# Second weights of the channel sub-layer in the buffers of the other half's input, loaded and split two steps ahead

## The chip, the cores and the metric

The kernel runs on one core of a Trainium2 chip. The metric is the device time of one execution in microseconds (us). A core has five engines that run their own instruction queues in order and wait for each other by semaphores: TensorE (PE in the profile; its weight loads are PEld), VectorE (DVE), ScalarE (ACT), GpSimd (POOL) and SyncE (SP), which here only issues transfers. Matrix products are accumulated in PSUM; everything else lies in SBUF.

## The reference

One layer of a decoder for 1024 prompt tokens and 8 sample tokens, each sample with 8192 cached positions. Its first sub-layer mixes tokens (stick-breaking attention, over a paged cache for the samples, and gated linear attention). Its second, the channel sub-layer, is the one that is changed:

```python
h2 = modulate(x1, sh2, sc2)                      # (tokens, 1024)
f = jnp.square(jax.nn.relu(h2 @ w_ff1)) @ w_ff2  # 1024 -> 4096 -> 1024
x2 = layer_norm(ALPHA * x1 + gt2 * f, ln2_g, ln2_b)
```

All arrays are float32.

## The kernel before, in words

**Products in three parts.** Each factor of a large product is split into a high part (a copy rounded to fp32r, by ACT, L313) and a low part (the rest, by POOL or DVE, L314), and the product is the sum of high x high, low x high and high x low. `three` puts the matmuls in that order, so a weight's low part is needed in the last third.

**The channel sub-layer** is `ffn(n, ...)`, run for the first half of the prompt (n = 0, 512 tokens) and then for the second (n = 1, with the 8 sample tokens beside it). The 4096 hidden units are 32 blocks of 128, taken in pairs. An *up* step (24 matmuls into `pmm`) makes one block's hidden values, which ACT evacuates (`rl`, L1502), DVE squares (L1503) and both split (`hidh`, `hidl`). A *down* step multiplies a pair's hidden values by two second weights: 4 token tiles x 2 halves of the columns, 6 matmuls each, in the PSUM tiles `pz` and `ptr`; DVE adds each to `f` (L1550). The steps go up, up, down, the down lagging one pair: A B | A' B' down(A,B) | A'' B'' down(A',B') ... The last down of a half is followed tile by tile by the gate (`tmpf`, L1554), the LayerNorm and the store; in the second half it takes four blocks, two of them in a wide buffer.

**Weights.** `load_split` fetches a block into a raw buffer by SP (`wf`, 512 KB), ACT writes its high part and POOL its low part. All of `raw` (6 buffers) and `whi` (3 buffers) are shared: first weights use a raw buffer, a high and a low one (the low ones are `raw` too), and so do second weights. Each step's weights are asked for while the step before is written out:

```python
        ws = yield from load(*steps[0])
        for y, (x, us) in enumerate(steps[:-1]):
            nxt = yield from load(*steps[y + 1])
```

**The input of the sub-layer.** `second_in(n, h2, alloc)` reads the first sub-layer's result back, normalizes it (L1382), transposes it on TensorE (`pT`), scales and shifts it (L1393) and splits it into 8 high and 8 low tiles. The first half's lie in the 16 buffers `b1`, the second half's in the 16 buffers `b2`. The second half's input is made as a task of its own soon after the first half's:

```python
        yield from mix_out(1, mhb, ws, lambda: flow.spawn(second_in(0, h2a, b1)))
        flow.spawn(second_in(1, h2b, b2), 60.0)
        yield from ffn(0, h2a, False)
```

**What sets the order.** The program is written out by generators whose tasks interleave by a clock counted in matmuls; a scheduler then orders each engine's instructions by that priority and by when buffers come free. The samples' attention over the cache runs as such tasks beside the first half's sub-layer: POOL issues the gathers of cache rows (`kt`, `vt`, 1 MB each, L636), DVE multiplies and reduces keys (L659, L661), TensorE multiplies values (`va`), and at the end transposes sums (`posT`, `pups`).

Of the kernel before, what the change touches and what calls it, by code (L numbers as in the profile page):

```python
# [12 lines left out]
F32R = mybir.dt.float32r  # L13
# [7 lines left out]
P = 128  # L21
# [14 lines left out]
A_LAG, A_PACE, B_LAG, SG_MAX = 6.5, 7.0, 2.0, 6  # L36
N_HK, N_MID, N_RAW, N_W, N_KV = 9, 9, 6, 3, 3
GATES_EARLY = 10
N_FA, N_DK = 8, 4
E_LAG = 2.0  # L40
U_LEAD = 7.2
SCALE = 1.2
# [74 lines left out]
def tile_trunk_step(ctx: ExitStack, tc: tile.TileContext, i: dict, o: dict):  # L117
# [4 lines left out]
    sb = ctx.enter_context(tc.tile_pool(name="sb", bufs=1))  # L122
# [8 lines left out]
    def fa(shape, name, dt=F32):  # L131
        return sb.tile(list(shape), dt, tag="fa", name=name, bufs=N_FA)

    def b1(name):
        return sb.tile([P, 512], F32R, tag="b1", name=name, bufs=16)

    def b2(name):
        return sb.tile([P, 512], F32R, tag="b2", name=name, bufs=16)

    def small(shape, name, dt=F32):  # L140
        return sb.tile(list(shape), dt, tag="small", name=name, bufs=5)
# [25 lines left out]
    flow = Flow()  # L167
# [83 lines left out]
    for c in range(2):  # L251
        t = cp.tile([P, 8], F32, name=f"sel2_{c}")
# [156 lines left out]
        yield 0.0  # L409


    hhi = [[(b1, b2)[n](f"hhi{k}_{n}") for n in range(2)] for k in range(8)]
    hlo = [[(b1, b2)[n](f"hlo{k}_{n}") for n in range(2)] for k in range(8)]
    hsT = cp.tile([P, 8, 32], F32, name="hsT")
    V.memset(hsT, 0.0)

# [772 lines left out]
    def mix_in(n):  # L1189

        ohl = []
        for x in range(2):
            for k in range(4):
                r = (hk if n else mid)([P, 512], "or")
                nc.sync.dma_start(r, d_o[x][k][n])
                h, lo = b1("oh"), b1("ol")
                split(r, h, lo, V)
                ohl.append((h, lo))
        return ohl

    def mix_up(n, ohl, mh):

        stage[0] = 2

        def fetch_up(m):
            r = raw([P, 2, 4, P], "ru")
            for x in range(2):
                fetch(r[:, x], w_up[x][:, P * m : P * m + P].rearrange("(k p) c -> p k c", p=P), U_LEAD)
            return r

        def load(m, r):
            wh = sb.tile([P, 2, 4, P], F32R, tag="whi", name="wuh", bufs=N_W)
            wl = sb.tile([P, 2, 4, P], F32R, tag="raw", name="wul", bufs=N_RAW)
            split(r, wh, wl)
            gs = []
            for x in range(2):
                g = hk([P, 512], "g")
                nc.sync.dma_start(g, d_br[x][m][n])
                gs.append(g)
            return wh, wl, gs  # L1220


        rr = [fetch_up(0)]
        nxt = load(0, rr[0])
        rr.append(fetch_up(1))
        for m in range(8):
            wh, wl, gs = nxt
            if m < 6:
                rr.append(fetch_up(m + 2))
            nxt = load(m + 1, rr[m + 1]) if m < 7 else wo_tiles(0)  # L1230
            for x in range(2):
                p = p_big(x)
                steps = three([(ohl[4 * x + k], (wh[:, x, k, :], wl[:, x, k, :])) for k in range(4)])
                for y, (h, wt) in enumerate(steps):
                    mm(p, wt, h, start=y == 0, stop=y == 11)
                    if y == 5:
                        yield
                V.tensor_tensor(gs[x], gs[x], p, ALU.mult)
                yield
            V.tensor_tensor(gs[0], gs[0], gs[1], ALU.add)  # L1240
            h, lo = b2("mh"), b2("ml")
            split(gs[0], h, lo)
            mh.append((h, lo))
        return nxt
# [130 lines left out]
    def second_in(n, h2, alloc):  # L1375

        for hf in range(2):
            xs = []
            for t in range(4):
                x = hk([P, 512], "x1")  # L1380
                nc.sync.dma_start(x, d_x1[4 * n + t][:, 512 * hf : 512 * hf + 512])
                V.tensor_scalar(  # L1382
                    x, x, x1_mu[:, 2 * t : 2 * t + 1, n], x1_mu[:, 2 * t + 1 : 2 * t + 2, n], ALU.subtract, ALU.mult
                )
                xs.append(x)
            yield 9.0
            for kk in range(4):
                k = 4 * hf + kk
                p = p_tr([P, 4, P], "pT2")
                for t in range(4):  # L1390
                    turn(p[:, t, :], xs[t][:, P * kk : P * kk + P], ident)
                t = hk([P, 512], "h2")
                V.tensor_scalar(  # L1393
                    t, p.rearrange("p a b -> p (a b)"), ada_col("sc2", k), ada_col("sh2", k), ALU.mult, ALU.add
                )
                h, lo = alloc("h2h"), alloc("h2l")
                split(t, h, lo)
                h2.append((h, lo))
                yield 1.5
        done.add(("h2", n))  # L1400

    def ffn(n, h2, smpl):


        NU = DFF // P
# [102 lines left out]
        def load_down(us):  # L1508
            ws = []
            wide = []  # L1510
            for x, u in enumerate(us):
                dst = None
                if x >= 2:
                    if not wide:
                        for nm in ("wwh", "wwl"):
                            wide.append(sb.tile([P, 2, 2, 512], F32R, tag="kv", name=nm, bufs=N_KV))
                    dst = wide[0][:, x - 2], wide[1][:, x - 2]
                go = hid[u][2]
                if go is not None:
                    yield lambda: bool(go)  # L1520

                def use(r, go=go):
                    held2.append(r)
                    if len(held2) == 2:
                        smp_down(held2, go)
                        held2.clear()

                ws.append(load_split(
                    w_ff2[P * u : P * u + P, :].rearrange("p (a b) -> p a b", a=2), 2, 512, "wf2",
                    None if go is None else use, dst,  # L1530
                ))
            return ws
# [33 lines left out]
        def load(x, us):  # L1566
            if us is None:
                return load_up(x)
            return (yield from load_down(us))
# [13 lines left out]
            store(y_s, xs, 8, nc.sync)  # L1583


        ws = yield from load(*steps[0])
        for y, (x, us) in enumerate(steps[:-1]):
            if smpl and y == len(steps) - 2:
                ln2 = rows(i["ln2_g"][0]), rows(i["ln2_b"][0])
                flow.spawn(smp_end())  # L1590
            nxt = yield from load(*steps[y + 1])
            if us is None:
                yield from up(x, *ws)
            else:
                for t in range(4):
                    for cc in range(2):
                        add_up(f[t][cc], down_tile(us, ws, t, cc), x == 0)
                        yield
            ws = nxt
        us = groups[-1]  # L1600
        for t in range(4):
            xs = halves(d_x1[4 * n + t], P, "xf")
            for h in range(2):
# [27 lines left out]
    def main():  # L1631
# [13 lines left out]
        yield from mix_out(0, mha, ws, lambda: o1.extend(mix_in(1)))  # L1645
        ws = yield from mix_up(1, o1, mhb)
        yield from mix_out(1, mhb, ws, lambda: flow.spawn(second_in(0, h2a, b1)))
        flow.spawn(second_in(1, h2b, b2), 60.0)
        yield from ffn(0, h2a, False)
        yield from ffn(1, h2b, True)  # L1650

# [75 lines left out]
```

## Time and profile before

| | |
|---|---|
| runs timed: median (lowest to highest of 3) | 2135.22 us (2133.79 to 2137.54) |
| the profiled execution, its own time | 2129.62 us |
| its span, first to last instruction | 2127.9 us |
| mean granted TensorE clock | 0.961 of full speed |
| busy: TensorE, its weight loads | 1954.9 us (92%), 1372.5 us |
| busy: VectorE, ScalarE, GpSimd | 1460.7, 709.9, 909.7 us |

The busy time is a sum over all stages. Engines wait at different places in each, so the stretches of the channel sub-layer (from about 1220 us) have to be read one by one; idle time of an engine that nobody waits for costs nothing.

### The profile page before, as it was taken

What the parts mean: (1) busy time and instruction counts of PE and PEld (TensorE: products, weight loads), DVE (VectorE), ACT (ScalarE), POOL (GpSimd) and SP (SyncE); (2) the same over time, 40 slices, a digit from 0 to 9 for tenths busy, and PEclk for the clock granted to TensorE, in tenths of its full rate; (3) what the DMA queues carried; (4) which work ended last, traced back from release to release, by engine and by line L of the source; (5) the groups of instructions that cost most, each with busy time, mean ns of one, the idle gap of its engine ahead of it and who ended that gap; (6) DMA issues with size and microseconds to landing.
All of it is one profiled execution on the core that took longest, in us unless ns stands there. A gap on an engine that the chain in (4) does not pass through costs nothing.

```text
span 2127.9 us, 28882 instructions
## 1 busy us (share of the span) xinstructions
PE 1954.9 (92%) x11300; PEld 1372.5 (64%) x11300; DVE 1460.7 (69%) x1770; ACT 709.9 (33%) x1152; POOL 909.7 (43%) x615
## 2 busy tenths in 40 slices
PE   5899999998899989888898889999999899999996
PEld 2776765665556656656876666676766666667774
DVE  6477888797777788656897989987335644333347
ACT  2333544553426533222232333222221432222222
POOL 2342233334334323327475657555444533234335
PEclk8998999999999889999999999999999999999998
DMA  7785578787778668798987888878668454443232
GB/s 263 245 303 179 183 259 271 254 272 265 264 260 297 224 206 301 283 343 287 338 316 259 279 275 299 284 281 300 206 203 279 147 159 125 134 132 106 80 99 102
DMA packets 270083, 498.06 MB, mean 234 GB/s; under 512 B 16006, under 2 KB 198630, under 8 KB 234107
## 3 DMA queue, kind: packets, MB, share of 16 engines
q0 software_dynamic: 36864, 268.45, 34.9%
q1 hardware_dynamic: 205538, 199.17, 29.7%
q10 hardware_dynamic: 27544, 28.59, 3.8%
q8 instruction: 89, 1.46, 0.3%
q14 instruction: 48, 0.39, 0.1%
HBM read 465.45 MB, written 30.71 MB: 233 GB/s over the span
## 4 chain that ended last, share of the span: by engine, by line
PE 49%; DVE 18%; DMA 14%; issue 11%; POOL 4%; ACT 3%; SPq 0%; DVEq 0%; ACTq 0%; POOLq 0%
PE pmm L189 21%; PE pz L189 7%; PE ptr L189 7%; DMA kt<-in_cache_k,idx 5%; DVE z L661 3%; PE pbig L189 3%; PE va L189 3%; DVE kt L659 3%; PE pfs L189 2%; DMA vt<-in_cache_v,idx 2%; DVE kp L772 2%; DMA wo<-in_w_o 1%; DMA wbr<-in_w_in 1%; DMA wf<-in_w_ff 1%; DVE xr L1299 1%
## 5 line engine op out<-in xcount | busy, mean ns | idle before, releaser
L659 DVE TENSOR_TENSOR kt<-kt,qb 128x2048 f32<-128x2048 f32 x128 | 291.5, 2278 | 80.9 <-DMA kt<-in_cache_k,idx 78.1
L661 DVE TENSOR_REDUCE z<-kt 128x32 f32<-128x2048 f32 x128 | 291.5, 2280 | 1.2
L636 POOL DMA_INDIRECT vt<-in_cache_v,idx x128 | 132.2, 1033 | 306.9 <-PE va L189 129.1
L636 POOL DMA_INDIRECT kt<-in_cache_k,idx x128 | 133.4, 1043 | 282.5 <-DVE z L661 102.0
L314 POOL TENSOR_TENSOR wfl<-wf,wfh 128x1024 fp32r<-128x1024 f32 x64 | 155.4, 2429 | 206.2 <-ACT wfh L313 187.5
L314 POOL TENSOR_TENSOR wf2l<-wf,wf2h 128x1024 fp32r<-128x1024 f32 x62 | 150.6, 2430 | 113.7 <-ACT wf2h L313 91.2
L313 ACT ACTIVATE wfh<-wf 128x1024 fp32r<-128x1024 f32 x64 | 67.5, 1055 | 269.5 <-PE ptr L189 142.4
L189 PE MATMUL pmm<-h2h,wfh 128*128 128x512 f32 x512 | 144.1, 415 | 11.7 <-DVE rl L1503 4.2
L189 PE MATMUL va<-vt,wT 128*8 128x512 f32 x1024 | 141.7, 619 | 13.7 <-DMA vt<-in_cache_v,idx 13.5
L189 PE MATMUL pmm<-h2l,wfh 128*128 128x512 f32 x512 | 137.5, 401 | 0.4 <-POOL h2l L314 0.4
L1503 DVE TENSOR_TENSOR rl<-rl,pmm 128x512 f32<-128x512 f32 x64 | 43.7, 682 | 134.8 <-ACT rl L1502 134.5
L189 PE MATMUL pmm<-h2h,wfl 128*128 128x512 f32 x512 | 132.5, 395 | 0.0
L189 PEld LDWEIGHTS pmm<-h2h,wfh 128*128 128x128 f32 x512 | 95.1, 194 | 56.9 <-issue 22.0
L1550 DVE TENSOR_TENSOR f<-f,pz 128x512 f32<-128x512 f32 x108 | 73.9, 684 | 70.5 <-PE pz L189 69.3
L189 PEld LDWEIGHTS pmm<-h2l,wfh 128*128 128x128 f32 x512 | 95.2, 189 | 31.1 <-issue 9.7
L189 PEld LDWEIGHTS pmm<-h2h,wfl 128*128 128x128 f32 x512 | 94.9, 188 | 26.1 <-issue 6.0
L1550 DVE TENSOR_TENSOR f<-f,ptr 128x512 f32<-128x512 f32 x108 | 73.9, 684 | 44.2 <-PE ptr L189 43.5
L772 DVE TENSOR_TENSOR_SCAN kp<-kp,zcol 128x512 f32<-128x512 f32 (+3 forms) x96 | 99.9, 1052 | 2.6 <-ACT kp L765 1.4
L189 PE MATMUL pz<-wf2h,hidh 128*128 128x512 f32 x248 | 83.5, 405 | 10.9 <-DVE tmpf L1554 4.5
L1502 ACT ACTIVATE rl<-pmm 128x512 f32<-128x512 f32 x64 | 38.2, 597 | 164.5 <-PE pmm L189 161.1
L314 DVE TENSOR_TENSOR hidl<-rl,hidh 128x512 fp32r<-128x512 f32 x64 | 79.0, 1234 | 15.9 <-ACT hidh L313 15.7
L189 PE MATMUL pz<-wf2l,hidh 128*128 128x512 f32 x248 | 82.1, 400 | 6.0 <-POOL wf2l L314 5.9
(431 smaller groups left out, 4248.0 us busy)
## 6 DMA issues: line engine op xcount, KB each, us to landing
wf<-in_w_ff SPq DMA_DIRECT2D x128, 512.0 KB
ra<-in_w_ada SPq DMA_DIRECT2D x24, 1024.0 KB
wfs<-in_w_ff SPq DMA_DIRECT2D x20, 512.0 KB
wbr<-in_w_in SPq DMA_DIRECT2D x16, 512.0 KB
d_br<-brg ACTq DMA_DIRECT2D x32, 256.0 KB
g<-d_br SPq DMA_DIRECT2D x32, 256.0 KB
wo<-in_w_o SPq DMA_DIRECT2D x16, 512.0 KB
xt<-in_x_prompt SPq DMA_DIRECT2D x8, 512.0 KB
```

The costliest lines, as they stand in the source:

```text
L189: ins = E.matmul(out, lhsT, rhs, start=start, stop=stop, **kw)
L313: S.activation(hi, src, AF.Copy)
L314: (eng or G).tensor_tensor(lo, src, hi.bitcast(F32), ALU.subtract)
L636: G.indirect_dma_start(t, None, src, bass.IndirectOffsetOnAxis(ap=idx[:, 16 * b + j : 16 * b + j + 1], axis=0))
L659: dot = V.tensor_tensor(k3, k3, qb[:, None, :].to_broadcast([P, 4, 512]), ALU.mult)
L661: V.tensor_reduce(z[:, :, :, j], kt.rearrange("p (r h d) -> p r h d", r=4, h=8), AX.X, ALU.add)
L772: V.tensor_tensor_scan(kp[:, 0:w][:, ::-1], kp[:, 0:w][:, ::-1], zcol.to_broadcast([P, w]), init, ALU.mult, ALU.max)
L1299: V.scalar_tensor_tensor(xr[t][hf][:, cs], xr[t][hf][:, cs], ALPHA, tmp, ALU.mult, ALU.add)
L1502: S.activation(rl, p, AF.Relu)
L1503: V.tensor_tensor(rl, rl, p, ALU.mult)
L1550: V.tensor_tensor(f, f, p, ALU.add)
```

## The change

The 16 single buffers of `b1` and of `b2` become 8 double ones each; inputs take a high and a low half of one. A second weight takes two of them (a whole one for its high part, one for its low): in the first half of the sub-layer from `b2`, for all pairs but the last three, in the second half from `b1`. Such a down step's weights are loaded and split two steps ahead, so together with those of the second up. The second half's input, which needs `b2`, is made when only the last three pairs of the first half are left.

```diff
-N_FA, N_DK = 8, 4
+N_FA, N_DK, N_LAST = 8, 4, 6
...
+    def pair(tag, name):
+
+        t = sb.tile([P, 2, 512], F32R, tag=tag, name=name, bufs=8)
+        return t[:, 0, :], t[:, 1, :]
+
     def b1(name):
-        return sb.tile([P, 512], F32R, tag="b1", name=name, bufs=16)
+        return pair("b1", name)
...
-                h, lo = alloc("h2h"), alloc("h2l")
+                h, lo = alloc("h2")
                 split(t, h, lo)
...
                 dst = None
+                if x < 2 and (n or us[0] < NU - N_LAST):
+
+                    dst = tuple(
+                        sb.tile([P, 2, 512], F32R, tag=("b2", "b1")[n], name=nm, bufs=8) for nm in ("wf2h", "wf2l")
+                    )
...
-        ws = yield from load(*steps[0])
+        ahead_ = [(yield from load(*steps[0]))]
+
+        def early(y):
+            us = steps[y][1] if y < len(steps) else None
+            return us is not None and len(us) == 2 and (n == 1 or us[0] < NU - N_LAST)
+
         for y, (x, us) in enumerate(steps[:-1]):
...
-            nxt = yield from load(*steps[y + 1])
+            while len(ahead_) < min(len(steps), y + (3 if early(y + 2) else 2)):
+                ahead_.append((yield from load(*steps[len(ahead_)])))
+            ws = ahead_[y]
+            if n == 0 and y == len(steps) - 3 * N_LAST // 2 + 1:
+                flow.spawn(second_in(1, h2b, b2))
...
-        flow.spawn(second_in(1, h2b, b2), 60.0)
         yield from ffn(0, h2a, False)
```

What it does to the order on the engines, at the three places that matter. First TensorE at the seam of the two halves: the last two token tiles of the first half's last down (`pz`, `ptr`), the cached values (`va`) and the first up of the second half (`pmm`). Before:

```order
L189 MATMUL pz<-wf2h,hidh 128x512 x2
L189 MATMUL pz<-wf2h,hidl 128x512 x2
L189 MATMUL pz<-wf2l,hidh 128x512 x2
L189 MATMUL ptr<-wf2h,hidh 128x512 x2
L189 MATMUL ptr<-wf2h,hidl 128x512 x2
L189 MATMUL ptr<-wf2l,hidh 128x512 x2
L189 MATMUL va<-vt,wT 8x512 x8
L189 MATMUL pmm<-h2h,wfh 128x512 x8
```

Now (the input's tiles are named `h`), after 16 matmuls of the up with `wfh`:

```order
L194 MATMUL pmm<-h_12769,wfl 128x512
L194 MATMUL pmm<-h_12802,wfl 128x512
L194 MATMUL pmm<-h_12822,wfl 128x512
L194 MATMUL pz<-wf2h,hidh 128x512 x2
L194 MATMUL pz<-wf2h,hidl 128x512 x2
L194 MATMUL pz<-wf2l,hidh 128x512 x2
L194 MATMUL ptr<-wf2h,hidh 128x512 x2
L194 MATMUL ptr<-wf2h,hidl 128x512 x2
L194 MATMUL ptr<-wf2l,hidh 128x512 x2
L194 MATMUL pmm<-h_12853,wfl 128x512
```

The 24 matmuls of the first up have moved ahead of the last two token tiles, 19 before the third and 5 before the fourth. Second ACT in the second half, one pair of blocks with the sample rows' partial sums (`partf`) between. Before:

```order
L313 ACTIVATE wfh<-wf 128x1024 x2
L1442 ACTIVATE partf<-pfs_14609 128x256
L1442 ACTIVATE partf<-pfs_14656 128x256
L1502 ACTIVATE rl<-pmm 128x512
L313 ACTIVATE hidh<-rl 128x512
L313 ACTIVATE wf2h<-wf_14692 128x1024
L1502 ACTIVATE rl<-pmm 128x512
L313 ACTIVATE wf2h<-wf_14698 128x1024
L313 ACTIVATE hidh<-rl 128x512
```

Now:

```order
L318 ACTIVATE wfh<-wf 128x1024
L1448 ACTIVATE partf<-pfs_14545 128x256
L318 ACTIVATE wf2h<-wf_14568 128x1024
L318 ACTIVATE wf2h<-wf_14574 128x1024
L1448 ACTIVATE partf<-pfs_14608 128x256
L1508 ACTIVATE rl<-pmm 128x512
L318 ACTIVATE hidh<-rl 128x512
L318 ACTIVATE wfh<-wf 128x1024
L1508 ACTIVATE rl<-pmm 128x512
L318 ACTIVATE hidh<-rl 128x512
```

Both high parts of the second weights now stand ahead of the up's evacuation and between the two `partf`; a first weight has moved behind it. Third DVE at the seam, behind the masked copy of the cached values' sum (`vz`). Before:

```order
L738 COPY_PREDICATED vz<-hmask,va 128x512
L304 RECIPROCAL rs<-rs 128x1
L1620 SCALAR_TENSOR_TENSOR nm<-mv,rs 128x1
L299 BN_STATS st<-f_10304 128x6
L299 BN_STATS st<-f_10305 128x6
L1623 TENSOR_TENSOR f_10302<-f_10302,row 128x512
L1623 TENSOR_TENSOR f_10303<-f_10303,row 128x512
L301 BN_AGGR mv<-st 128x2
L1503 TENSOR_TENSOR rl<-rl,pmm 128x512
```

Now:

```order
L744 COPY_PREDICATED vz<-hmask,va 128x512
L309 RECIPROCAL rs<-rs 128x1
L1639 SCALAR_TENSOR_TENSOR nm<-mv,rs 128x1
L304 BN_STATS st<-f_10250 128x6
L304 BN_STATS st<-f_10251 128x6
L1509 TENSOR_TENSOR rl<-rl,pmm 128x512
L1642 TENSOR_TENSOR f_10248<-f_10248,row 128x512
L1642 TENSOR_TENSOR f_10249<-f_10249,row 128x512
```

The product that frees the first up's accumulator (`rl<-rl,pmm`) has moved ahead of the two products with the gain `row`.

## Rows read from the trace of the kernel before

**Rows 1.** The page, busy time of each engine (share of the span) and instructions.

```profile
PE 1954.9 (92%) x11300; PEld 1372.5 (64%) x11300; DVE 1460.7 (69%) x1770; ACT 709.9 (33%) x1152; POOL 909.7 (43%) x615
```

**Rows 2.** Stretches: us, busy time per engine, granted clock, DMA share, GB/s.

```profile
core 0: us, PE busy (x) PEld busy (x) DVE busy (x) ACT busy (x) POOL busy (x), PEclk, DMA share, GB/s
...
1220.00:1500.00 280.00, 265.17 (x1218) 186.43 (x1216) 239.20 (x228) 83.80 (x113) 161.66 (x103) 0.98 0.83 287
1500.00:1640.00 140.00, 140.00 (x670) 96.78 (x670) 54.50 (x78) 34.04 (x43) 68.60 (x40) 1.00 0.67 226
1640.00:1690.00 50.00, 40.64 (x187) 28.72 (x185) 41.77 (x64) 18.80 (x28) 28.81 (x15) 0.93 0.52 164
1690.00:1780.00 90.00, 84.75 (x423) 60.62 (x424) 38.35 (x60) 28.85 (x45) 32.75 (x15) 1.00 0.47 145
1780.00:1930.00 150.00, 146.17 (x912) 101.94 (x911) 49.42 (x89) 35.74 (x50) 47.65 (x20) 1.00 0.43 137
1930.00:2080.00 150.00, 150.00 (x813) 110.58 (x812) 53.43 (x91) 40.71 (x53) 57.82 (x25) 1.00 0.30 95
```

**Rows 3.** Waits of PE, 1220:2128: us in total, times, longest us.

```profile
PE pz L189 <- POOL wf2l L314: 5.9, 7, 1.1
PE pz L189 <- DVE tmpf L1554: 4.5, 3, 2.2
PE va L189 <- DMA vt<-in_cache_v,idx: 4.5, 3, 3.0
PE pz L189 <- DVE f L1550: 4.3, 2, 2.4
...
PE pz L189 <- ACT wf2h L313: 2.0, 3, 0.7
PE pfs L189 <- DMA wf<-in_w_ff: 2.0, 5, 0.7
```

**Rows 4.** Waits of all engines, 1220:2128.

```profile
POOL wfl L314 <- ACT wfh L313: 187.5, 35, 12.3
...
ACT wfh L313 <- PE ptr L189: 142.4, 19, 11.9
```

**Rows 5.** Instructions in order of time, 1742:1752: start, us, engine [idle before].

```profile
1746.97 0.60 ACT L1502 ACTIVATE rl<-pmm 128x512 f32<-128x512 f32 x1 [3.74 <-PE pmm L189]
...
1747.46 1.05 ACT L313 ACTIVATE wf2h<-wf 128x1024 fp32r<-128x1024 f32 x1
...
1748.56 0.50 PE L189 MATMUL pz<-wf2h,hidh 128*128 128x512 f32 x1 [0.70 <-ACT wf2h L313]
...
1751.01 0.50 PE L189 MATMUL pz<-wf2l,hidh 128*128 128x512 f32 x1 [1.02 <-POOL wf2l L314]
```

**Rows 6.** Groups of DVE, 1240:1340: busy us, mean ns, idle before.

```profile
L1393 DVE TENSOR_SCALAR h<-pT,adaT 128x512 f32<-128x512 f32 x8 | 6.4, 806 | 3.0 <-POOL wf2l L314 2.4 <-PE pT L213 0.6
...
L1382 DVE TENSOR_SCALAR x<-x,x_mu 128x512 f32<-128x512 f32 x8 | 4.3, 598 | 0.0
```

**Rows 7.** Groups of PE, 1240:1340.

```profile
L213 PE MATMUL pT<-ident,x 128*128 128x128 f32 x32 | 4.8, 274 | 0.0
```

**Rows 8.** Instructions in order of time, 1660:1676.

```profile
1668.92 1.05 PE L189 MATMUL posT<-ones,vz 128*128 128x1 f32 x8 [2.07 <-DVE vz L738]
...
1672.05 1.27 DVE L1623 TENSOR_TENSOR f<-f,row 128x512 f32<-128x512 f32 x2
...
1673.36 0.63 DVE L1503 TENSOR_TENSOR rl<-rl,pmm 128x512 f32<-128x512 f32 x1
...
1674.14 2.47 PE L189 MATMUL pmm<-h2h,wfh 128*128 128x512 f32 x5 [4.17 <-DVE osT L743]
```

**Rows 9.** The chain that ended last, 1500:1512: one up.

```profile
1504.34 5.56 PE pmm L189 x24
```

**Rows 10.** Waits of all engines, 1780:1930.

```profile
ACT wfh L313 <- DMA wf<-in_w_ff: 71.9, 10, 13.6
```

**Rows 11.** Line L1604, DVE: duration ns min/median/max.

```profile
L1604 DVE TENSOR_TENSOR f<-f,gmt x8: 684/693/2741, 1629.9 to 2067.6; 128x512 f32<-128x512 f32 x8
```

More of the change, by code (lines that the diff above doesn't have):

```diff
@@ L132, in fa @@
         return sb.tile(list(shape), dt, tag="fa", name=name, bufs=N_FA)
+    def pair(tag, name):
+        t = sb.tile([P, 2, 512], F32R, tag=tag, name=name, bufs=8)
+        return t[:, 0, :], t[:, 1, :]
     def b1(name):
-        return sb.tile([P, 512], F32R, tag="b1", name=name, bufs=16)
+        return pair("b1", name)
     def b2(name):
-        return sb.tile([P, 512], F32R, tag="b2", name=name, bufs=16)
+        return pair("b2", name)
     def small(shape, name, dt=F32):
@@ L409, in ada @@
         yield 0.0
-    hhi = [[(b1, b2)[n](f"hhi{k}_{n}") for n in range(2)] for k in range(8)]
-    hlo = [[(b1, b2)[n](f"hlo{k}_{n}") for n in range(2)] for k in range(8)]
+    hhl = [[(b1, b2)[n](f"hhl{k}_{n}") for n in range(2)] for k in range(8)]
+    hhi = [[x[0] for x in y] for y in hhl]
+    hlo = [[x[1] for x in y] for y in hhl]
     hsT = cp.tile([P, 8, 32], F32, name="hsT")
@@ L1195, in mix_in @@
                 nc.sync.dma_start(r, d_o[x][k][n])
-                h, lo = b1("oh"), b1("ol")
+                h, lo = b1("ohl")
                 split(r, h, lo, V)
@@ L1240, in mix_up @@
             V.tensor_tensor(gs[0], gs[0], gs[1], ALU.add)
-            h, lo = b2("mh"), b2("ml")
+            h, lo = b2("mhl")
             split(gs[0], h, lo)
@@ L1598, in ffn @@
                         yield
-            ws = nxt
-        us = groups[-1]
+        us, ws = groups[-1], ahead_[-1]
         for t in range(4):
```

## Prediction

> **What bounds the kernel now.** I read the page first, then the stretches of the channel sub-layer one by one, then who waits for whom in them. TensorE is busy 1954.9 us of a span of 2127.9 us [rows 1], so what any change to waits can win is small. The channel sub-layer is the last part, from about 1220 us on. Its stretches [rows 2] are to be read by the difference between their length and TensorE's busy time: 14.8 us idle in 1220:1500, where VectorE is busy 239.2 us of 280 with the cached keys; none in 1500:1640; 9.4 us in 1640:1690, where the first half's closing LayerNorm fills VectorE; 5.2 us in 1690:1780; 3.8 us in 1780:1930; none in 1930:2080. That is 33.2 us, plus the tail after 2080, which the change does not touch. So no more than some 33 us can be won here, and nothing in the 290 us of 1500:1640 and 1930:2080, where the splits are late on their engines but never late for TensorE.
>
> Who ends these idle times stands in TensorE's waits [rows 3]: 5.9 us for the low part of a second weight (POOL), 2.0 us for its high part (ACT), 4.5 us for rows of the cached values, 4.5 us for the gated sum, 4.3 us for the sum into f, 2.0 us for the raw first weights of the sample rows. The other engines' waits [rows 4] look far larger (ACT stood 142.4 us before a first weight's high part until a down tile was done, POOL 187.5 us behind it), but they are mostly time in which nothing was needed; only what reaches TensorE counts.
>
> One case in full [rows 5]: the second unit's high part starts on ACT at 1747.46, directly behind the evacuation of the up at 1746.97, because its buffer is shared with the first weights and ACT meets it late. TensorE stands 0.70 us for it at 1748.56, and 1.02 us for the low part, which POOL can only begin then, at 1751.01. A pair like this costs about 1.7 us where it happens at all; there are ten such waits in the whole sub-layer (7 and 3 in rows 3).
>
> **The change part by part.**
>
> *Second weights into buffers of their own, split a step earlier (term A).* No instruction is added or removed. 26 of the 32 second weights of the first half and 30 of the second half leave the two small pools for the eight double buffers of the other half, and their load and split are issued before the first up of the pair instead of before the second, one up of 24 matmuls earlier, 5.56 us [rows 9]. Each of the ten waits is at most 1.1 us, so 5.6 us of lead covers all of them, and the order on ACT shows both high parts ahead of the up's evacuation. I take all of 5.9 + 2.0 = **-7.9 us**. The lower bound of the gain is half of it, 4 us: where VectorE or a cache load is late at the same place, TensorE stops again at the next instruction, as it does at 1748.56 and again at 1751.01. More than 7.9 us cannot come from this wait.
>
> *The second half's input is made later (terms B and C).* It leaves 1250:1330 for the last quarter of the first half. VectorE loses 6.4 + 4.3 = 10.7 us of work there [rows 6]. TensorE's waits for VectorE's sums and for cached values, 4.3 + 4.5 = 8.8 us over the sub-layer [rows 3], are what this can shorten; the work leaves only 80 of the 280 us of that stretch, so I take a quarter, **B = -2 us**, between 0 and -8.8. Its 32 transposes occupy TensorE 4.8 us [rows 7]. Where they stood TensorE was idle for 5% [rows 2]; where they go (1500:1640) it never is. If the old place was paced by VectorE they gave nothing back, and the cost is 4.8 us; if by TensorE, nothing. The old place is much nearer the second: **C = +1 us**, between 0 and +4.8. The 8 splits and the two passes of VectorE go to a stretch where POOL was busy 68.6 and VectorE 54.5 of 140 us, and hide there; if that cover were gone, an evacuation of 0.8 us each would stand before the next transpose, 6.4 us. The buffers are free in time: the last group that holds them ends one step after the task begins, and three groups follow.
>
> *The seam between the halves (term D).* TensorE's first up of the second half is now partly issued between the last two pairs of down tiles (first piece of order). That fills the waits for the gated sums, but not more: TensorE then comes to the transposed sum of the cached values (posT) sooner and waits there, since VectorE's closing chain is the same. In the trace TensorE waits 2.07 us there and again until 1674.14, when VectorE's product for the first up, begun at 1673.36, has freed an accumulator [rows 8]. In the new order that product stands ahead of the two products with the LayerNorm's gain, 1.27 us [rows 8], so the second wait ends that much sooner: **D = -1.3 us**, between 0 and -4.5, the whole wait for the gated sum.
>
> *Room for raw weights (term E).* A second weight's low part no longer takes one of the six raw buffers, so a pair of steps needs six of them and not eight, and first weights can be fetched sooner. TensorE's wait for raw first weights is 2.0 us [rows 3]; I take half, **E = -1 us**, between 0 and -2.
>
> *Pairs of buffers.* High and low part of one input are now freed together; the high part is the last one read anyway, so this costs nothing before 1220 us, and the order there differs in a few neighbouring places only.
>
> Sum: -7.9 - 2 + 1 - 1.3 - 1 = **-11.2 us**. The profiled execution took 2129.62 us, 1.72 us more than its span, so it would take 2118.4 us. The runs timed have their median at 2135.22 us, 5.6 us above; the difference carries over: **2124.0 us**.
>
> **The rivals.**
>
> *The waits change their name.* In 1220:1500 VectorE is busy 85% of the time and sets the pace with the cache; then what is won on the weights there is lost to the next sum or cache load: A falls to its lower bound, B is nothing and C is its upper end. What is left is 4 + 1.3 + 1 - 4.8 = 1.5 us: 2133.7 us. For it speaks that the two waits at 1748.56 and 1751.01 show how one late thing follows another; against it, that VectorE had 40.8 us idle in that stretch.
>
> *The queues run free.* ACT's 142.4 us and POOL's 187.5 us [rows 4] stand ahead of the cache loads that POOL issues. If these loads come sooner once nothing stands in POOL's queue, the waits for cached values and sums go wholly (8.8 us instead of 2), and the granted clock of that stretch, 0.98 [rows 2], gives back up to 2% of 280 us, 5.6 us; I count half: -11.2 - 6.8 - 2.8 = -20.8, 2114.4 us. Against it: POOL's own waits for the cache are on VectorE and TensorE too, which the change leaves.
>
> *ACT waits for a load with evacuations behind it (slower).* In the new order two high parts stand on ACT between the two evacuations of the sample rows' sums (partf) and ahead of the up's evacuation (second piece of order). Their only wait is their own load. In 1780:1930 ACT waited 71.9 us in 10 times for raw weights, at most 13.6 us [rows 10]. One up covers 5.56 us of that [rows 9]. If the second weights' loads come as late as the first weights' did, between the mean (7.2) and the longest, about 10.4 us, TensorE loses 4.8 us in each of the five pairs of that stretch, 24 us: 2148 us. It decides against the change from 5.56 + 11.2 / 5 = 7.8 us of lateness. Against it: these loads now ask for fewer buffers, and it needs all five pairs.
>
> *POOL and VectorE collide at the seam.* A gain product of VectorE took 2741 ns instead of the median 693 while POOL split a weight [rows 11], 2.05 us more. The first two first weights of the second half are now split before the closing LayerNorm's additions, so two such meetings may fall into VectorE's chain: -11.2 + 4.1 = -7.1, 2128.1 us. The Trainium skill has this as a rule (SBUF — State Buffer, "SBUF: two separate sides"): VectorE and GpSimd share a port pair under an exclusive lock, and whoever starts first keeps it for the whole instruction. By that rule each meeting could cost up to the split's own length; the row above shows such a case, but not what fixes its size.
>
> *The change does nothing,* since the lead is eaten by raw buffers that come free no sooner: A and E vanish and B, C and D leave 2.3 us, 2132.9 us. I count it with the first rival.
>
> **How the numbers follow.** Forecast (gain 5 to 17 us) 0.48; waits change their name, or nothing 0.22; queues run free 0.12; ACT behind a load 0.10; collision at the seam 0.08. The forecast's own range is 2118 to 2131 us (its terms at their ends, without the extremes of B). The range of 8 in 10 takes in the free queues below and the first rival above and leaves out the slow one: 2111 to 2137 us. A measurement of this kernel tells 0.2%, 4.3 us, from no change. Faster than that: the forecast nearly whole (0.45), the free queues (0.12), the seam (0.07) and a third of the first rival (0.07), together 0.71; within: 0.17, the rest of the first rival and the edge of the forecast; slower: 0.12, nearly all from ACT.
>
> **What would show it.** A: no wait of TensorE for a second weight's parts except in the first half's last three groups, and ACT's 142.4 us before first weights gone. B: fewer waits on sums between 1220 and 1500. C: transposes between 1500 and 1640 with TensorE still without idle time. D: the posT wait as before or longer, the one after it shorter. E: no wait on raw first weights. The prediction is wrong if TensorE's idle time in 1220:1500 stays at 15 us, or if ACT shows waits for a second weight's load with partf or an evacuation behind it.

## The result

The changed kernel took 2118.73 us (median of 7 runs, 2113.58 to 2132.62), the kernel before 2132.93 us in the runs beside it (2131.02 to 2137.54): ratio 0.9938, 95% interval 0.9912 to 0.9963, some 13 us faster. A second comparison, beside other kernels, gave 0.9966 (0.9942 to 0.9991). Both intervals lie below 1, so it is faster, by 0.6 and by 0.3%; the changed kernel's own times scatter over 19 and 22 us.

### The profile page after: what moved, and what is told of

Its sections match the earlier page's. It is cut to its first block, busy times and chain, and to the rows that moved or that the text cites. A ratio compares the mean times of both kernels' runs of the same rounds, so it can differ in the third digit from the quotient of the medians.

```text
span 2117.0 us, 28820 instructions
## 1 busy us (share of the span) xinstructions
PE 1946.5 (92%) x11300; PEld 1379.9 (65%) x11300; DVE 1459.9 (69%) x1770; ACT 710.7 (34%) x1152; POOL 907.1 (43%) x615
## 5 line engine op out<-in xcount | busy, mean ns | idle before, releaser
L194 PE MATMUL pmm<-h,wfh 128*128 128x512 f32 x1024 | 269.9, 409 | 10.1 <-DVE rl L1509 6.2
L194 PEld LDWEIGHTS pmm<-h,wfh 128*128 128x128 f32 x1024 | 192.2, 193 | 83.6 <-issue 25.4
L194 PE MATMUL pmm<-hhl,wbrh 128*128 128x512 f32 x512 | 143.7, 420 | 0.0
L194 PE MATMUL pmm<-h,wfl 128*128 128x512 f32 x512 | 133.1, 396 | 0.0
L194 PEld LDWEIGHTS pmm<-hhl,wbrh 128*128 128x128 f32 x512 | 95.0, 197 | 34.5 <-issue 16.9
L194 PEld LDWEIGHTS pmm<-h,wfl 128*128 128x128 f32 x512 | 94.6, 188 | 30.2 <-issue 8.7
L194 PE MATMUL ptr<-wf2h,hidh 128*128 128x512 f32 x248 | 81.0, 408 | 11.3 <-DVE f L1561 10.7
L318 ACT ACTIVATE wf2h<-wf 128x1024 fp32r<-128x1024 f32 x62 | 65.3, 1053 | 60.8 <-DMA wf<-in_w_ff 47.1
L194 PE MATMUL pbig<-woh,mhl 128*128 128x256 f32 x512 | 72.5, 290 | 11.8 <-DVE rs L309 5.0
```

The source lines that it names most:

```text
L194: ins = E.matmul(out, lhsT, rhs, start=start, stop=stop, **kw)
L318: S.activation(hi, src, AF.Copy)
```

## The profile after

The profiled execution took 2118.73 us with a span of 2117.0 us, 10.9 us less than the span before. The page's busy line answers to [rows 1]: TensorE is busy 8.4 us less with the same instructions.

```profile
PE 1946.5 (92%) x11300; PEld 1379.9 (65%) x11300; DVE 1459.9 (69%) x1770; ACT 710.7 (34%) x1152; POOL 907.1 (43%) x615
```

The stretches, columns as in [rows 2]:

```profile
1220.00:1500.00 280.00, 263.83 (x1209) 186.44 (x1208) 222.54 (x216) 85.94 (x114) 165.76 (x101) 0.98 0.83 292
1500.00:1640.00 140.00, 140.00 (x684) 97.93 (x681) 62.31 (x88) 34.55 (x46) 66.69 (x43) 1.00 0.63 211
1640.00:1690.00 50.00, 41.38 (x180) 29.86 (x179) 47.22 (x67) 17.44 (x24) 27.20 (x14) 0.86 0.66 217
1690.00:1780.00 90.00, 87.94 (x450) 64.35 (x449) 42.83 (x61) 32.87 (x51) 39.23 (x18) 1.00 0.52 156
1780.00:1930.00 150.00, 149.12 (x934) 108.25 (x933) 50.05 (x95) 36.63 (x50) 48.37 (x21) 1.00 0.44 134
1930.00:2080.00 150.00, 149.95 (x841) 113.40 (x840) 68.55 (x103) 42.15 (x57) 58.00 (x24) 1.00 0.33 99
```

TensorE's idle time fell in 1690:1930 (from 9.1 to 2.9 us) and rose in 1220:1500 (from 14.8 to 16.2). In 1930:2080 it is "busy" throughout as before, but issued 841 matmuls there and not 813. TensorE's waits from 1220 us on, answering to [rows 3]:

```profile
PE ptr L194 <- DVE f L1561: 10.7, 3, 6.2
PE pmm L194 <- DVE rl L1509: 6.2, 2, 4.2
PE posT L194 <- DVE vz L744: 5.9, 1, 5.9
PE psT L218 <- DVE srow L315: 2.0, 1, 2.0
PE pfs L194 <- DMA wf<-in_w_ff: 0.8, 2, 0.4
PE pz L194 <- POOL wf2l L319: 0.7, 1, 0.7
...
PE va L194 <- DMA vt<-in_cache_v,idx: 0.2, 1, 0.2
```

The ten waits for second weights (7.9 us) have become one of 0.7 us, in the first half's last group. At the top stand waits for sums into `f`, 10.7 us in three times (`ptr`), of which there were 1.2 us before; of the 6.2 us for `rl`, a wait of 4.2 us was there before too. The waits of the other engines, answering to [rows 4], say what took the place of the old ones: ACT's waits before first weights until a down tile is done (142.4 us in 19 times) are down to 2.1 us, once; it waits for loads.

```profile
DVE rl L1509 <- ACT rl L1508: 145.0, 45, 11.7
POOL wfl L319 <- ACT wfh L318: 138.8, 24, 12.8
ACT wfh L318 <- DMA wf<-in_w_ff: 120.2, 28, 13.8
...
ACT wfh L318 <- PE pmm L194: 87.4, 9, 14.5
...
ACT wf2h L318 <- DMA wf<-in_w_ff: 47.1, 27, 3.2
...
ACT wfh L318 <- PE ptr L194: 2.1, 1, 2.1
```

**Where the 10.9 us come from.** I cut both traces at three events that each has: the first `hidh`, the first gated product of the first half (`tmpf`) and the first gated product of the second.

```text
                       before    after    difference
up to the first hidh   1217.5   1224.9    +7.4
first half              428.8    429.9    +1.1
second half             452.0    432.0   -20.0
tail                     29.6     30.2    +0.6
```

So nearly the whole gain is made in the second half. Ten matmuls of its first up, 2.3 us, stand ahead of the cut wherever the input is made late, so -20.0 and +1.1 are rather -17.7 and -1.2. TensorE's idle time in the second half is 7.5 us less (18.4 to 10.9, summed over the matmuls' starts and ends). The other 10 us are time in which both traces call it busy. 3.0 us of them are in the matmuls of the down tiles. From start to start each takes 231 ns where nothing holds it up; over the second half they take 7.4 us more than that before, and 4.4 us more after. Two stretches in order of time show the largest part, 5.5 us. The first is of the kernel before: the samples' products with the second weights of a pair (`smp_down`: four products, eight records, each product into another quarter of the array's columns) stand in two places, with three matmuls of an up between.

```profile
1969.05 1.05 PE L189 MATMUL pfs<-wf,hs 128*32 128x512 f32 x4
1970.03 0.96 PE L189 MATMUL pmm<-h2h,wfh 128*128 128x512 f32 x3
1970.92 1.05 PE L189 MATMUL pfs<-wf,hs 128*32 128x512 f32 x4
1971.90 1.43 PE L189 MATMUL pmm<-h2h,wfh 128*128 128x512 f32 x5
```

After the change both weights are there at once, and the four stand together:

```profile
1961.13 1.04 PE L194 MATMUL pfs<-wf,hs 128*32 128x512 f32 x8
1962.11 1.65 PE L194 MATMUL pmm<-h,wfh 128*128 128x512 f32 x6
```

From start to the next start, four records took 0.98 us (1969.05 to 1970.03), and eight take 0.98 us too: the products run side by side if nothing stands between them. Over the second half the 128 records took 26.0 us and now 20.6. The Trainium skill (TensorEngine Tiling (Array Packing), "Tiling Modes") says that different tiles of the array can run matmuls in parallel, and that changing the tiling mode drains the engine. The trace agrees with the first part by these numbers; the 1.0 us less for the products of `cT` and 0.5 us less for those of `partf`, with fewer changes between kinds of products, fit the second without proving it.

**What took the first half's gain.** One place in order of time, after the change:

```profile
1480.33 0.38 SPq L324 DMA_DIRECT2D wf<-in_w_ff  x1
...
1485.00 0.64 PE L194 MATMUL pz<-wf2h,hidh 128*128 128x512 f32 x2
...
1491.34 1.06 ACT L318 ACTIVATE wfh<-wf 128x1024 fp32r<-128x1024 f32 x1 [9.92 <-DMA wf<-in_w_ff]
1492.30 0.58 ACT L1508 ACTIVATE rl<-pmm 128x512 f32<-128x512 f32 x1
...
1492.91 0.69 DVE L1509 TENSOR_TENSOR rl<-rl,pmm 128x512 f32<-128x512 f32 x1 [11.72 <-ACT rl L1508]
1493.51 0.68 DVE L1561 TENSOR_TENSOR f<-f,pz 128x512 f32<-128x512 f32 x1
...
1496.03 1.22 PE L194 MATMUL ptr<-wf2h,hidh 128*128 128x512 f32 x2 [6.24 <-DVE f L1561]
```

TensorE finished the up at 1485 and went on with down tiles. ACT stood 9.92 us for the load of the *next* pair's first weight (asked for at 1480.33, 10.9 us before it landed), with this up's evacuation behind it; VectorE stood for the evacuation, with the sums into `f` behind it; TensorE ran out of accumulators and stood 6.24 us. Over the 32 ups of the first half I add how long each `rl` starts after the last matmul of an up that ended before it, and each `hidh` after its product on VectorE: 5.3 us in the trace before, 25.1 us after. That sum is "late" in the table below. Where the next up already runs on TensorE it leaves the lateness of `rl` out; counted from each up's own last matmul the sums are 18.4 and 31.3 us, and 4.9 and 22.0 us without the first three ups, which are late in nearly every trace.

## The experiments

Each was profiled and timed against the kernel before. Halves are cut as above, in us (with the input late, 2.3 us of the second lie in the first); idle is TensorE's idle time in the first half, clock its mean granted clock there. Each row's halves are those of one execution.

```text
                         ratio (95% interval)     first   second  late   idle  clock
before                   1                        428.8   452.0   5.3    16.3  0.988
the change               0.9938 (0.9912, 0.9963)  429.9   432.0   25.1   16.9  0.988
the change, again        0.9966 (0.9942, 0.9991)  440.8   434.4   31.1   22.6  0.973
second half only         0.9910 (0.9877, 0.9942)  424.6   438.2   5.1    13.2  0.988
first half only          1.0055 (1.0031, 1.0078)  441.0   453.5   30.0   20.8  0.965
fours in before          1.0004 (0.9980, 1.0027)  425.4   456.5   4.9    14.1  0.988
one ahead                0.9908 (0.9873, 0.9943)  433.2   431.4   21.6   16.4  0.980
relu on VectorE          1.0011 (0.9986, 1.0037)  443.9   434.9   17.7*  26.5  0.981
input late alone         0.9984 (0.9968, 1.0000)  425.6   452.4   5.7    13.1  0.992
order held               0.9923 (0.9895, 0.9950)  425.6   437.9   8.4    11.6  0.996
order held, one ahead    0.9944 (0.9923, 0.9966)  432.0   436.4   11.9   15.6  0.992
late input, second half  0.9902 (0.9865, 0.9938)  422.9   435.8   5.6    12.1  0.996
order held, first half   0.9901 (0.9868, 0.9935)  427.1   434.6   8.8    12.8  0.996
twos in the change       0.9998 (0.9977, 1.0020)  440.7   441.6   30.4   20.7  0.965
* hidh alone
```

**The second half only.**

```diff
-                if x < 2 and (n or us[0] < NU - N_LAST):
+                if x < 2 and n:            # and early() likewise; second_in(1) where it was before
```

> The edit is made in the second half alone (own buffers and two steps of lead for ffn(1)); ffn(0) and the place of the second half's input are those of before. Theory 1 (what the two traces now suggest): all of the gain is made in the second half, where the profiled executions took 452.0 and 432.1 us from the first gated product of the first half to that of the second; so this kernel is as fast as the whole change or faster, ratio 0.990 to 0.994 (about 2113 to 2120 us), and its profile shows 20 us less in that stretch. Rival (the prediction on record): the waits for second weights are spread over both halves, and the second half has 5.4 of 7.9 us of them; then this gives -5.4 - 1.3 - 1, about -8 us, ratio 0.996.

As fast as the whole change or faster, as theory 1 has it; its second half is 13.8 us shorter and not 20 (2.3 us of that are the cut), its first half 4.2. At the same place the first weight's load is asked for at 1483.43, 3 us later than in the change; but the evacuation stands ahead of the split, and TensorE has no wait between 1480 and 1510:

```profile
1489.93 0.66 ACT L1508 ACTIVATE rl<-pmm 128x512 f32<-128x512 f32 x1
...
1492.57 1.05 ACT L318 ACTIVATE wfh<-wf 128x1024 fp32r<-128x1024 f32 x1
```

**The first half only** (the same edit with `n == 0`, the input late).

> The edit is made in the first half alone (own buffers, two steps of lead, the second half's input moved late); the second weights of ffn(1) go through the shared buffers, one step ahead. Theory 1: what the second weights gain in the first half is lost again where ACT waits for a raw weight with the evacuation of an up behind it (a 6.2 us and a 4.2 us wait of TensorE in the profile of the changed kernel); ratio 0.998 to 1.004, and TensorE shows such waits on sums and on rl in this profile too. Rival (the prediction on record): waits of 2.5 us gone, VectorE relieved, transposes paid for: -2.5 - 2 + 1, ratio 0.998, without waits of several us.

Slower by some 12 us. TensorE's waits in 1220:1640:

```profile
PE ptr L194 <- DVE f L1561: 12.0, 4, 7.1
PE pmm L194 <- DVE rl L1509: 4.2, 1, 4.2
PE pz L194 <- DVE f L1561: 3.0, 2, 2.5
```

The waits for second weights (2.5 us before) are gone, those for sums take 15.0 us (3.6 before; the wait of 4.2 us for `rl` is that of before). The theory's mechanism holds; its price was set too low, since it counted the waits alone. The granted clock of this first half is 0.965 and not 0.988, and what that costs is worked out below, at the change's second profile.

**Four products together, in the kernel before.**

```diff
-            for y in range(2):
+            for y in (1, 0):               # in smp_down: the later load first
```

> The kernel before with one line changed: smp_down issues the products of its second weight before those of its first, so that all four 32-column products wait for the same, later load and stand together in TensorE's order. Theory 1: four of them side by side take 0.98 us like two, so the 26.0 us that these products took in the kernel before fall to about 20 us or less and each saved break of an up saves 0.2 us more: 5 to 9 us, ratio 0.9958 to 0.9977, with no change in the waits for second weights. Rival: bringing them together is free or costs (they wait for the later load at the place of the first two, up to 1 us each time): ratio 0.999 to 1.003.

The products fell from 26.0 to 19.6 us as expected, but the time did not. What was won came back as waits for second weights, which rose from 5.9 to 10.8 us (low parts) and from 2.0 to 3.4 us (high parts):

```profile
PE pz L189 <- POOL wf2l L314: 10.8, 10, 1.4
...
PE pz L189 <- ACT wf2h L313: 3.4, 7, 0.9
```

The last two stretches of its windows, beside [rows 2], show where:

```profile
1780.00:1930.00 150.00, 139.16 (x873) 97.52 (x873) 40.33 (x81) 35.14 (x49) 45.21 (x19) 0.98 0.42 134
1930.00:2080.00 150.00, 150.00 (x839) 114.95 (x838) 56.15 (x95) 42.05 (x54) 59.90 (x25) 1.00 0.31 99
```

In 1930:2080 it issued 839 matmuls and not 813, the gain. In 1780:1930 TensorE's idle time grew from 3.8 to 10.8 us, its waits for second weights there from 1.7 to 8.3, and the granted clock fell from 1.00 to 0.98: there the second weights set the pace, and work taken off TensorE alone comes back as waits.

**One step ahead** (`early` returns False: own buffers, no lead).

> The changed kernel without the lead: second weights lie in the other half's buffers, but each load is issued one step ahead as before. Theory 1: the buffers of their own do the work, since ACT then meets no buffer that a down tile still holds and its order is nearly that of the changed kernel: ratio as the whole change, 0.992 to 0.997, with at most 2 us of waits for second weights. Rival: the step of lead does it; the waits for second weights stay at 5 to 8 us and the ratio is 0.997 to 1.0.

As fast as the whole change, with 0.7 us of waits for second weights: the buffers do it, not the step of lead. The first half's lateness, 21.6 us, comes with the buffers too.

**Relu on VectorE in the first half.**

```diff
-            S.activation(rl, p, AF.Relu)
+            if n:
+                S.activation(rl, p, AF.Relu)
+            else:
+                V.tensor_scalar(rl, p, 0.0, None, ALU.max)
```

> The changed kernel, but in the first half VectorE and not ACT takes the relu of an up's sum out of the accumulator (32 instructions more on VectorE at about 0.67 us, 32 fewer on ACT). Theory (from the four runs so far): in the first half of the changed kernel ACT waits for a raw weight with the evacuation of a finished up behind it (evacuations come 16.3 us late in all, against 2.6 us before); with the evacuation on another engine that wait no longer reaches the sums, and the first half, 430 to 441 us in the profiles, falls to 425 us or less; ratio 0.986 to 0.991. Rival: VectorE, about 80% busy there, gets 21 us more work and becomes the bound; the sums come later for that, the first half stays at 430 us or grows, ratio 0.993 to 1.0.

The rival: the first half takes 443.9 us. VectorE has more work in it, and `hidh`, still on ACT, is 17.7 us late behind loads. It tells nothing of the evacuations alone.

**The later input alone** (`early` False, no buffers of their own).

> Of the change only the pairs and the later place of the second half's input; all second weights go through the shared buffers, one step ahead. Theory: ACT's order around the evacuations stays that of before, so nothing comes late by loads; the first half gains up to 2 us where VectorE is relieved and loses up to 5 us for the transposes at their new place; the second half keeps its 452 us; ratio 0.999 to 1.003. Rival: the later input is itself what costs the first half, then the ratio is that of the run with the first half alone, 1.004 to 1.007.

No loss by it, rather a gain of 3 us (0 to 7). In 1220:1640 TensorE no longer waits for sums into `f` (3.6 us before), and 2.4 us and not 4.5 for cached values; its waits for second weights are 5.4 us there and not 2.5.

**The order held on ACT.**

```diff
+            not_before(ins, after)          # in split: ins writes the high part
...
+        split(r, h, lo, None, last_rl[0])   # in load_split
...
+            last_rl[0] = S.activation(rl, p, AF.Relu).ins.name
```

> The changed kernel with an order on ACT: no split of a weight may stand ahead of the evacuation of an up that was issued before it. That puts the next group's first weights behind the last evacuation; but with two steps of lead both second weights now stand ahead of the evacuation of the group's first up. Theory: only the first weights' lateness is cured and the second weights' takes its place where their loads are late: evacuations 5 to 16 us late in all in the first half, ratio 0.989 to 0.996. Rival: second weights are never late enough; then evacuations are under 4 us late, ratio 0.986 to 0.990.

> As the run before with the loads only one step ahead, so that neither first nor second weights stand ahead of an evacuation that is due earlier. Theory: evacuations are under 4 us late in all in the first half, as in the kernel before; the first half takes 424 to 429 us and the second 431 to 434 us; ratio 0.985 to 0.990, the fastest so far. Rival: what costs the first half is something else that the later input brings; then it stays at 433 us as in the run with the load one step ahead, ratio 0.991.

With the lead the first half falls to 425.6 us (late 8.4, of it 1.6 for the evacuations), while the second rises to 437.9, with a wait of 2.6 us for `hidh` at a place where the change had none. Without the lead I expected the fastest kernel and was wrong: 432.0 us. The evacuations are only 1.4 us late there, but `hidh`, which I had not held ahead of anything, is 10.5 us late.

**The change again, and two versions put together from these runs.** In the first of them second weights have buffers of their own in the second half alone and the input is late; in the other the order on ACT is held for `n == 0` alone.

> The changed kernel once more, beside the runs it is to be compared with. Theory: its first half ends late where loads come late (evacuations 10 us or more late in all, the longest behind a split of first weights that waits for its load), its second half takes 431 to 434 us as in the first profile, since nothing waits for loads there; ratio 0.991 to 0.996. Rival: the lateness in the first profile was that execution's own; then evacuations are under 4 us late here and the first half takes 425 us.

> Second weights in buffers of their own and two steps ahead in the second half alone, with the second half's input at its later place; in the first half second weights go through the shared buffers one step ahead. Theory: ACT's order in the first half keeps the evacuations ahead of the splits, so it takes 424 to 428 us with evacuations under 4 us late, and the second half 431 to 434 us; ratio 0.986 to 0.990, faster than the whole change. Rival: the first half profits from the early weights more than it loses by ACT's order, then this is no faster than the whole change, 0.992 to 0.996.

> The changed kernel, with no split ahead of the last evacuation issued, in the first half alone. Theory: the first half as in the run with the order held in both halves (425.6 us, evacuations 1.6 us late), the second half as in the changed kernel (432 us); ratio 0.986 to 0.990. Rival: the order held moves other waits in (the first weights of the next up), the first half stays at 430 us and the ratio is that of the whole change, 0.992 to 0.996.

Both end at 2115 to 2116 us, beside 2128.08 us of the change in the same set of runs, and 2135.42 us of the kernel before: 12 to 13 us faster than the change, 19 to 20 us faster than before. Their intervals, and those of the second half only and of one ahead, overlap; which of the four is best I can't tell, and beside the change's first comparison (0.9938) theirs overlap too. The change's second profile shows a second victim of the same order: `hidh`.

```profile
1324.85 0.69 DVE L1509 TENSOR_TENSOR rl<-rl,pmm 128x512 f32<-128x512 f32 x1 [3.84 <-ACT rl L1508]
...
1330.34 1.06 ACT L318 ACTIVATE wfh<-wf 128x1024 fp32r<-128x1024 f32 x1 [5.52 <-DMA wf<-in_w_ff]
...
1331.95 2.42 DVE L319 TENSOR_TENSOR hidl<-rl,hidh 128x512 fp32r<-128x512 f32 x1 [5.65 <-ACT hidh L318]
...
1335.02 1.22 PE L194 MATMUL ptr<-wf2h,hidh 128*128 128x512 f32 x2 [6.23 <-DVE f L1561]
```

ACT waits 5.52 us for a load with `hidh` behind, VectorE waits for `hidh` in front of its sums, TensorE for a sum. In the first profile the load came 2.65 us late at this place. Between the eighth `hidh` and the eleventh the two profiles part by 8 us, and with the step before it by 11, which is the difference of their first halves.

About half of that is the clock. The two profiles from 1334 to 1344 us, the second one first:

```profile
1334.00:1344.00 10.00, 8.98 (x21) 4.27 (x22) 3.38 (x5) 2.32 (x3) 3.57 (x2) 0.50 0.23 61
1334.00:1344.00 10.00, 10.00 (x50) 7.03 (x47) 5.00 (x8) 0.00 (x0) 1.90 (x2) 1.00 0.42 142
```

Where TensorE had stood 6.23 us, the granted clock was 0.50, the lower of its two levels (1.2 and not 2.4 GHz), and it issued 21 matmuls; in the first profile, where it had stood 3.36 us, the clock was 1.00 and it issued 50. From start to start a matmul of 128x512 takes 427 ns at the lower level and 231 ns at the upper (medians of the traces), so 46% of the busy time at the lower level is lost. In the first half TensorE was busy at that level for 18.5 us in the second profile and for 7.1 us in the first: 5.2 us, by this estimate, and with 5.7 us more of idle time that is the 10.9 us between them. The same sum for the first half only, beside before, is 4.5 us of idle time, 5.9 us by the clock (23.0 and 10.2 us busy at the lower level) and the 2.3 us of the ten matmuls, 12.7 us in all, where 12.2 us were measured.

**Two and two, in the changed kernel** (the second weight's two products are spawned one step of the planner's clock later).

> The changed kernel with the four 32-column products of each pair of second weights issued as two and two, the second two 1 step of the planner's clock later, behind other work of TensorE. Theory: two of them take as long as four, 0.98 us, so the 20.6 us of these products become 26 to 31 us, and the second half takes 437 to 444 us instead of 432; ratio 0.994 to 1.0. Rival: the products' time was covered (the second half is paced by its weights): second half 432 to 434 us, ratio as the whole change.

```profile
1972.91 1.03 PE L194 MATMUL pfs<-wf,hs 128*32 128x512 f32 x4
1973.87 1.67 PE L194 MATMUL pmm<-h,wfh 128*128 128x512 f32 x6
1975.46 1.05 PE L194 MATMUL pfs<-wf,hs 128*32 128x512 f32 x4
```

The products take 27.3 us and not 20.6, those of `cT` 2.5 us more, and the second half 441.6 us, with the same idle time. With the second weights out of the way, this work sets the time, and its place in the order is worth 7 to 10 us against the two profiles of the change.

## Why the prediction was right, and which steps were not

The time forecast, 2124.0 us, is 0.5% below the median it started from; the two comparisons measured 0.6 and 0.3%. The number held, but partly by luck. Its terms put -7.7 us into the second half (D, E and 5.4 us of A) and -3.5 us into the first; the profiles show -17.7 and -1.2, and +7.4 us ahead of the first `hidh`, where it had nothing. What it missed on either side, some 10 us, nearly cancels.

- **Term A** (-7.9 us of waits) held: 7.2 us of them are gone, and the one left is in a group that the prediction had excepted. Its reason was half right. The lead of one up did nothing that the buffers alone do not do (one ahead).
- **Terms B and C** (-2 + 1 us) are borne out where they stand alone, 0.9984 with an interval that takes in both them and no change at all. In 1500:1640 TensorE has no idle time with the 32 transposes in it, as predicted. In the whole change B failed: waits on sums in 1220:1500 did not fall (3.6 us before, 11.2 after), and TensorE's idle time there stayed at 16 us, which the prediction had named as the sign of an error.
- **Term D** (-1.3 us) held: posT's wait rose from 2.1 to 5.9 us, the one behind it fell from 4.2 to 2.0 (its row names the copy `osT` before, right behind the product that the prediction read, and the product itself after), and 2.7 us of waits for gated sums at the seam are gone; 9.0 before, 7.9 after.
- **Term E** (-1 us) held: raw first weights of the sample rows, 2.0 to 0.8 us.
- **The step that failed** is that nothing could be won where TensorE is always busy ("nothing in the 290 us of 1500:1640 and 1930:2080"). There the order of its work was worth something: in 1930:2080 and the stretches ahead of it 5.5 us by products that run side by side, 1.5 us by `cT` and `partf` and 3.0 us by down tiles that are held up less.
- **The rival that came true in the wrong place** is ACT behind a load. I looked for it in 1780:1930, with second weights and `partf`; it came in the first half, with first weights ahead of `rl` and `hidh`. The order of the changed kernel showed it, had I read the first half's ups as well as the second's. The first half alone measures its price with all else it brings: +12 us, of which some 6 are the granted clock behind the stops; the prediction had the clock only as a gain. Its sign did show in 1780:1930, and cost nothing there: ACT waited nine times for a second weight's load, 3.2 us at most, which is less than the 7.8 us from which the prediction had it decide, and TensorE was idle for 0.9 us of that stretch.

```profile
ACT wf2h L318 <- DMA wf<-in_w_ff: 18.7, 9, 3.2
```

- **The other rivals.** That VectorE's pace takes the gain back was not seen: VectorE's waits in the first half are for ACT. Of the free queues a part came: the waits for cached values fell from 4.5 to 0.2 us, but those for sums rose, and the clock of 1220:1500 stayed at 0.98.
- **The collision at the seam came**, and in the rival's size. The closing additions before, and after:

```profile
1641.50 4.90 DVE L1605 SCALAR_TENSOR_TENSOR f<-xf,f 128x512 f32<-128x512 f32 x8
```

```profile
1644.55 2.38 POOL L319 TENSOR_TENSOR wf2l<-wf,wf2h 128x1024 fp32r<-128x1024 f32 x1 [5.07 <-issue]
1644.73 2.75 DVE L1623 TENSOR_TENSOR f<-f,gmt 128x512 f32<-128x512 f32 x1
...
1647.41 7.50 DVE L1624 SCALAR_TENSOR_TENSOR f<-xf,f 128x512 f32<-128x512 f32 x8
1648.34 2.40 POOL L319 TENSOR_TENSOR wfl<-wf,wfh 128x1024 fp32r<-128x1024 f32 x1
```

Beside POOL's split of a first weight one addition took 3.28 us (median 0.68), so the eight take 2.6 us longer; beside its splits of second weights two gain products took 1.93 and 2.75 us, where before one took 2.74. That is 3.8 us more on VectorE; the rival had 4.1. The long addition is in all eleven profiles with the late input and in none of the three without it. `posT` waits 5.9 to 7.2 us in the eleven and 1.3 to 2.6 us in the three; the up that comes sooner is a reason for that too, so what the collision costs TensorE is not shown.

What stays open: the first `hidh` comes at 1217.5 and 1214.1 us in the two profiles of the order before, and at 1214.9 to 1229.8 us in the twelve with pairs of buffers. Part of this goes with the granted clock ahead of it: 0.940 to 0.942 in the three that come last, 0.952 to 0.954 in the three that come first. Whether the pairs cost a few microseconds there, where I had put nothing, these runs don't settle.

## What to carry to other kernels

When a change moves loads ahead, read the order of the engine that prepares them: whatever stands behind an instruction that waits for a transfer inherits that transfer's lateness, and an evacuation there stops the accumulators. A stop of TensorE can cost more than its length: read the granted clock behind it as well. A busy engine is not a floor: look at what its time is spent on, and whether small products that could run side by side stand together. And a saving on one engine shows only where the next thing in line, here the second weights, doesn't set the pace.

## What I had not expected of the hardware

Four 32-column products take the same 0.98 us as two. And the changed kernel's times scatter (2113.3 to 2134.9 us over 12 runs) more than the difference to be measured: a load that came 5.52 us late in one execution and 2.65 us in another decided some 8 to 11 us, through three queues that each keep their order and, for about half of it, through the granted clock: 0.50 behind TensorE's stop of 6.23 us, 1.00 behind that of 3.36 us.
